# Pseudo-random shifts of the recorded priorities in a planned two-layer trunk kernel

## The chip, the cores and the metric

The kernel runs on one core of a Trainium2 chip. The metric is the device time of one execution in microseconds; the time of a version is the median of its runs. The kernel is one program, planned as a whole before it is emitted: a Python planner decides in which order each engine gets its instructions, and the chip only executes the queues.

## What is computed

Two layers over 1024 tokens of width 1024. Layer 0 mixes tokens by sparse attention (an indexer scores all keys, the 256 best of each query are kept, 16 query heads share 4 key heads); layer 1 mixes them by a gated convolution of width 3. Each mixer is followed by a SwiGLU block of hidden size 2816, and each sublayer has an RMS norm whose shift, scale and gate come from a conditioning vector.

```
def reference(x, c, positions, ada_w, ada_b, ...):
    c_act = jax.nn.silu(c)
    for i in range(DEPTH):
        mod = c_act @ ada_w[i] + ada_b[i]
        sh1, sc1, g1, sh2, sc2, g2 = [m[:, None, :] for m in jnp.split(mod, 6, axis=-1)]
        h = _rmsnorm(x, norm1_g[i]) * (1.0 + sc1) + sh1
        if i % N_MIXERS == 0:
            y = _dsa_mixer(h, positions, ...)
        else:
            y = _short_conv_mixer(h, conv_w_in[j], conv_w[j], conv_w_out[j])
        x = x + g1 * y
        h = _rmsnorm(x, norm2_g[i]) * (1.0 + sc2) + sh2
        x = x + g2 * _swiglu(h, ffn_w_gate[i], ffn_w_up[i], ffn_w_down[i])
    return x
```

## The kernel before

**What is recorded.** Every instruction is first recorded as an `Op` with an estimated cost, its dependences and a priority. 16,676 of them are recorded, in program order. Until the attention is done (up to recorded operation 5433, with a few exceptions) the priority is a due time in estimated microseconds, which the code sets by hand in `plan.pri`: projections are spaced 6.2 apart, attention blocks by `t_att`. In everything after that, the tail, `plan.pri` is None and the priority is the operation's own number, so that an earlier recorded operation goes first.

**What sets the order.** `drain` keeps an estimated clock for each engine. Again and again it takes the engine that could start something earliest and gives it, of the operations whose inputs are ready by that estimated clock, the one of the lowest priority (`choice` may prefer, on TensorE, one that keeps the array's tile shape, within 4.0 of priority). Since readiness comes from the estimated clock, one operation that moves shifts the clock of its engine a little, and later picks fall differently, also among operations whose own priority has not changed. Some PSUM copies may go to ScalarE or VectorE; `drain` decides that too. The order found is what the five hardware queues get, and each queue is worked off in that order. SyncE (SP) issues nearly all DMAs, so a DMA that waits for its buffer holds those behind it.

**How the matmuls are done.** A float32 product is three matmuls: operands are split into a high and a low part (`split`: ScalarE casts `whi`, VectorE subtracts for `wlo`), and `mm3` multiplies hi*hi, hi*lo, lo*hi. In the tail each product of two 2x2 blocked matrices is done with seven block products instead of eight (`Pair.done` for the weights of the convolution, gate and up; `down_pairs` for down). For one `Pair` SP loads two weight tiles `raw` (there are two buffers), VectorE forms sums of their blocks (`s<-raw`, `s<-raw,s`), ScalarE and VectorE split each sum into `whi` and `wlo`, TensorE runs 12 matmuls of 128x512 for each of the seven products, and VectorE adds the products up (`u`, `v`, `cv`). A `raw` buffer is free for the next load when its last sum has been formed. In `conv` VectorE also runs the taps of the convolution on the same tiles, as operations with `vec` as an input. `norm_stat` sums squares over eight tiles on VectorE (`u<-u`), then TensorE transposes the sum (`ps_mm<-ident,u`); its matmuls and those of the neighbouring products stand in one TensorE queue.

**Stages by time in the profile.** Startup, norm and positions to about 100 us; projections and indexer to 297; attention to about 600; output projection and first FFN gate/up to about 1085; down to 1290; convolution to 1500; its output projection to 1590; second FFN to the end.

Of the kernel before, what the change touches and what calls it, by code (L numbers as in the profile page):

```python
# [185 lines left out]
class Plan:  # L186
# [7 lines left out]
    CHANGE = {(ROWS, None): 0.285, (None, ROWS): 0.115, (None, COLS): 0.12, (COLS, None): 0.15,  # L194
              (ROWS, COLS): 0.277, (COLS, ROWS): 0.278}
    TRAIL = 1.0 / 450e3
    STAY = 4.0

    def __init__(self, nc, tc):
# [89 lines left out]
    def matmuls(self, calls, rate, start=True, stop=True):  # L289

        kw = {"start": start, "stop": stop}
        emits = [self.emitter("tensor", "matmul", c, kw) for c in calls]

        def emit():
            for e in emits:
                e()

        self.count += 1
        op = Op("tensor", rate * calls[0][0].free, emit, (self.pri, self.count))
        op.form = tuple(calls[0][1].shape)  # L300
        outs = [c[0] for c in calls]
        self.note(op, [r for c in calls for r in c], outs)
        return op

    def record(self, eng, fn, args, kw, other=None):
        vals = list(args) + list(kw.values())
        outs = [kw["out"] if "out" in kw else args[0]]
        if "accum_out" in kw:
            outs.append(kw["accum_out"])
        refs = [v for v in vals if isinstance(v, Ref)]  # L310
        ins = [v for v in refs if not any(v is o for o in outs)]
        emit = self.emitter(eng, fn, args, kw)
        shaped = outs[0] if isinstance(outs[0], Ref) else refs[0]
        func = {"func": args[2]} if fn == "activation" else {}
        cost, lat = self.cost(eng, fn, shaped, ins, {**kw, **func})
        self.count += 1
        pri = (self.count if self.pri is None else self.pri, self.count)
        op = Op(eng, cost, emit, pri, lat)
        if "accum_out" in kw:
            op.late = 0.13 if eng == "vector" else 0.1  # L320
        if other is not None:
            op.other = (other[0], self.cost(*other[:2], shaped, ins, kw)[0],
                        self.emitter(*other, args, kw))
        if fn == "dma_start":
            op.lat = lat + shaped.free * shaped.shape[0] * 4 / 380e3
        self.note(op, refs, outs)
        return op
# [110 lines left out]
    def choice(self, e):  # L438

        now = self.now[e]  # L440
        if e == "tensor" and now[0][1].form != self.form:
            same = [v for v in now if v[1].form == self.form and v[1].end is None
                    and not v[1].parked and v[0][0] < now[0][0][0] + self.STAY]
            if same:
# [41 lines left out]
    def drain(self, *pools):  # L486

        held = []
        while any(p.pending for p in pools) if pools else True:
# [36 lines left out]
            if op.lat:  # L526
                self.dma = max(self.dma, end) + (op.lat - 1.6)
                end = self.dma + 1.6 + (op.lat - 1.6) * 380e3 * self.TRAIL
                if e == "sync":
# [1452 lines left out]
```

## Time and profile before

| what | value |
|---|---|
| time, median of 3 runs | 2274.2 us (2271.48 to 2274.24) |
| the profiled execution | 2273.65 us, span 2271.9 us, granted clock 0.985 |
| instructions in the profile | 32575 |
| VectorE busy | 1903.7 us (84%) |
| ScalarE busy | 1141.0 us (50%) |
| DMA | 353.72 MB, 156 GB/s on average |

The profile's page gives busy time by engine, the chain of work that ended last, and groups of instructions. A view by windows gives the same for stretches of the span: for each engine the busy time and, in brackets, the number of instructions, then the clock that TensorE was granted. All instructions have the line of the one emitting helper (L276), so tiles tell them apart: `ps_g<-t,whi` writes a PSUM tile `ps_g` from the operands `t` and `whi`. PE is TensorE, DVE VectorE, ACT ScalarE, SP SyncE.

### The profile page before, as it was taken

How to read it: one execution, taken by the hardware profiler on the slowest of the kernel's cores; microseconds unless marked ns; L12 is line 12 of the kernel's file. 1: busy time of each engine (PE TensorE's matmuls, PEld its weight loads, DVE VectorE, ACT ScalarE, POOL GpSimd, SP SyncE). 2: the span in 40 equal slices, each digit the busy share in tenths (PEclk: the TensorE clock that was granted, in tenths of full speed). 3: DMA queues.
4: the chain of work that ended last, by engine and by line, in shares of the span. 5: the costliest groups of instructions: out<-in, count | busy, mean ns of one | idle time of the engine just before them, and what ended most of it. 6: DMA issues, size and time to landing. Idle time of an engine off the chain costs nothing.

```text
span 2271.9 us, 32575 instructions
## 1 busy us (share of the span) xinstructions
PE 2199.9 (97%) x11435; PEld 1779.5 (78%) x11435; DVE 1903.7 (84%) x3828; ACT 1141.0 (50%) x2163; POOL 5.2 (0%) x19
## 2 busy tenths in 40 slices
PE   3999999999999999999999999999999999999999
PEld 3757866876888778888888787887887888888887
DVE  7889999798599989887898998986788887767974
ACT  5587899767654323333445552224553333334444
POOL 0000000000000000000000000000000000000000
PEclk6999989999999999999999999999999999999999
DMA  9313333542354665455972354234445532349824
GB/s 309 122 48 89 97 94 107 161 142 96 110 162 123 222 195 183 147 165 177 389 280 85 122 156 138 86 115 158 121 120 177 157 121 89 125 140 382 290 87 139
DMA packets 332317, 353.72 MB, mean 156 GB/s; under 512 B 19289, under 2 KB 216954, under 8 KB 332154
## 3 DMA queue, kind: packets, MB, share of 16 engines
q1 hardware_dynamic: 331944, 351.52, 47.7%
q8 instruction: 89, 1.46, 0.3%
q14 instruction: 74, 0.61, 0.1%
q10 hardware_dynamic: 210, 0.14, 0.0%
HBM read 278.97 MB, written 68.94 MB: 153 GB/s over the span
## 4 chain that ended last, share of the span: by engine, by line
PE 78%; DVE 10%; issue 3%; ACT 2%; DMA 1%; POOL 0%; ACTq 0%; DVEq 0%; POOLq 0%
PE ps_g L276 45%; PE ps_mm L276 31%; PE ps_o L276 2%; DVE u L276 2%; DVE wlo L276 1%; PE ps_L L276 1%; DVE s L276 1%; DVE sc L276 1%; DMA adaw<-in_ada_w_dram 1%; DVE p L276 1%; DVE karena L276 1%; DVE adacc L276 1%; ACT p L276 1%; ACT junk L276 1%; ACT pf L276 0%
## 5 line engine op out<-in xcount | busy, mean ns | idle before, releaser
L276 ACT CAST whi<-raw 128x512 fp32r<-128x512 f32 (+1 forms) x313 | 192.5, 619 | 392.2 <-PE ps_g L276 142.2
L276 PE MATMUL ps_g<-t,whi 128*128 128x512 f32 x1184 | 367.6, 391 | 3.6 <-ACT whi L276 3.6
L276 PE MATMUL ps_g<-h,whi 128*128 128x512 f32 x1056 | 326.3, 390 | 0.5 <-ACT whi L276 0.5
L276 ACT CAST whi<-s 128x512 fp32r<-128x512 f32 x276 | 170.5, 621 | 305.7 <-DVE s L276 130.9
L276 DVE TENSOR_TENSOR wlo<-raw,whi 128x512 fp32r<-128x512 f32 (+1 forms) x314 | 214.3, 684 | 80.7 <-ACT whi L276 80.6
L276 PEld LDWEIGHTS ps_g<-t,whi 128*128 128x128 f32 x1184 | 223.0, 189 | 51.3 <-ACT whi L276 5.3
L276 PE MATMUL ps_g<-t,wlo 128*128 128x512 f32 x592 | 231.6, 392 | 3.5 <-DVE wlo L276 3.3
L276 PEld LDWEIGHTS ps_g<-h,whi 128*128 128x128 f32 x1056 | 197.6, 188 | 41.9 <-ACT whi L276 1.4
L276 PE MATMUL ps_g<-h,wlo 128*128 128x512 f32 x528 | 205.9, 390 | 1.6 <-DVE wlo L276 1.6
L276 DVE TENSOR_TENSOR wlo<-s,whi 128x512 fp32r<-128x512 f32 x276 | 187.4, 684 | 17.3 <-ACT whi L276 16.8
L276 PE MATMUL ps_mm<-t,whi 128*128 128x512 f32 x608 | 189.5, 392 | 1.7 <-ACT whi L276 1.7
L276 PE MATMUL ps_g<-ph,whi 128*128 128x512 f32 x572 | 179.1, 389 | 0.0
L276 PEld LDWEIGHTS ps_mm<-t,whi 128*128 128x128 f32 x608 | 114.8, 189 | 26.4 <-ACT whi L276 2.8
L276 PEld LDWEIGHTS ps_g<-t,wlo 128*128 128x128 f32 x592 | 111.7, 189 | 29.3 <-DVE wlo L276 6.0
L276 PEld LDWEIGHTS ps_g<-ph,whi 128*128 128x128 f32 x572 | 107.4, 188 | 22.3
L276 PE MATMUL ps_mm<-t,wlo 128*128 128x512 f32 x304 | 119.8, 394 | 2.5 <-DVE wlo L276 2.5
L276 ACT ACTIVATE junk<-sc,bs 128x384 bf16<-128x384 f32 (+3 forms) x124 | 109.9, 887 | 15.8 <-DVE bs L276 7.7
L276 PEld LDWEIGHTS ps_g<-h,wlo 128*128 128x128 f32 x528 | 99.1, 188 | 22.7 <-DVE wlo L276 2.1
L276 DVE TENSOR_TENSOR u<-u 128x512 f32<-128x512 f32 x170 | 114.1, 683 | 1.8 <-ACT u L276 0.8
L276 DVE SCALAR_TENSOR_TENSOR adacc<-adaw,cact,adacc 128x512 f32<-128x512 f32 x140 | 104.2, 744 | 8.5 <-DMA adaw<-in_ada_w_dram 8.0
L276 PE MATMUL ps_g<-ph,wlo 128*128 128x512 f32 x286 | 110.3, 389 | 0.0
L276 PE MATMUL ps_mm<-hhi,whi 128*128 128x512 f32 (+2 forms) x240 | 93.5, 391 | 4.7 <-ACT hhi L276 3.1
(310 smaller groups left out, 4769.3 us busy)
## 6 DMA issues: line engine op xcount, KB each, us to landing
adaw<-in_ada_w_dram SPq DMA_DIRECT2D x160, 256.0 KB, 2.9
ph<-in_ffn_w_down_dram SPq DMA_DIRECT2D x66, 512.0 KB, 6.5
raw<-in_ffn_w_gate_dram SPq DMA_DIRECT2D x54, 512.0 KB, 4.2
raw<-in_ffn_w_up_dram SPq DMA_DIRECT2D x54, 512.0 KB, 4.1
raw<-in_conv_w_in_dram SPq DMA_DIRECT2D x34, 512.0 KB, 4.6
raw<-in_ffn_w_down_dram SPq DMA_DIRECT2D x44, 256.0 KB, 2.6
ph<-in_ffn_w_down_dram SPq DMA_DIRECT2D x44, 256.0 KB, 4.3
raw<-in_attn_w_in_dram SPq DMA_DIRECT2D x18, 512.0 KB, 3.7
```

Source lines behind the costliest of these rows:

```text
L276: f(*[a.get() if isinstance(a, Ref) else a for a in args], **{k: a.get() if isinstance(a, Ref) else a for k, a in kw.items()})
```

## The change

A table of 123 seeds is added, one for each hundred recorded operations; 29 of them are not zero, and from operation 12,300 on there is none. Where the seed of its hundred is not zero, an operation's priority gets a fixed pseudo-random amount added: up to 4.0 either way in the tail, that is four places of the recorded order, and up to 0.5 either way where the priority is a due time. Nothing is computed differently, and the operations and their dependences are the same.

```
+    SPAN = 100
+    SHAKE = (0, 824, 0, 0, 0, 657, 0, 545, 0, 210, 0, 0, 0, 0, 0, 240, 0, 214, 0, 0, 0, 0, 0,
...
-        self.count += 1
-        op = Op("tensor", rate * calls[0][0].free, emit, (self.pri, self.count))
+        op = Op("tensor", rate * calls[0][0].free, emit, self.rank())
...
+    def rank(self):
+
+        self.count += 1
+        i, at = self.count // self.SPAN, self.count if self.pri is None else self.pri
+        seed = self.SHAKE[i] if i < len(self.SHAKE) else 0
+        if seed:
+            x = ((self.count * 7919 + seed * 104729) * 2654435761 >> 13) % 1024 / 512.0 - 1.0
+            at += x * (4.0 if self.pri is None else 0.5)
+        return at, self.count
...
-        self.count += 1
-        pri = (self.count if self.pri is None else self.pri, self.count)
-        op = Op(eng, cost, emit, pri, lat)
+        op = Op(eng, cost, emit, self.rank(), lat)
```

What the planner makes of it, over both programs: 2,897 operations have another priority; by the longest common order of each queue, 511 of 10,083 operations stand elsewhere on TensorE, 982 of 3,558 on VectorE, 357 of 1,897 on ScalarE and 66 of 1,123 on SyncE; 26 copies change engine (15 from VectorE to ScalarE, 11 the other way). On TensorE and SyncE nothing is moved after about operation 13,300 (about 1,780 us), nor on SyncE between recorded operations 6,046 and 10,101 (about 650 to 1,296 us).

The helper's line is 276 before and 283 after. Three places follow.

VectorE in the convolution, before: from the sums of one `Pair` to the last of them (1384.0 to 1390.6 us in the profile). `s` are sums of weight blocks and `wlo` low parts, `vec` marks the taps.

```order
L276 TENSOR_SCALAR u<-u,vec 128x512
L276 COPY u<-u 128x2
L276 TENSOR_TENSOR s<-raw,s 128x512
L276 SCALAR_TENSOR_TENSOR u<-u,vec 128x512
L276 TENSOR_TENSOR u<-u 128x512
L276 SCALAR_TENSOR_TENSOR u<-u,vec 128x512
L276 TENSOR_SCALAR u<-u,vec 128x512
L276 TENSOR_TENSOR wlo<-s,whi 128x512
L276 SCALAR_TENSOR_TENSOR u<-u,vec 128x512
L276 TENSOR_TENSOR wlo<-s,whi 128x512
L276 SCALAR_TENSOR_TENSOR u<-u,vec 128x512
L276 TENSOR_TENSOR s<-raw 128x512
```

The same `Pair` on VectorE after the change, from its first sum on:

```order
L283 TENSOR_TENSOR s<-raw 128x512 x2
L283 TENSOR_TENSOR u<-cv,ps_mm 128x512
L283 TENSOR_TENSOR wlo<-raw,whi 128x512
L283 TENSOR_TENSOR v<-u 128x512
L283 TENSOR_TENSOR wlo<-s,whi 128x512
L283 TENSOR_TENSOR v<-v,ps_g 128x512
L283 TENSOR_TENSOR s<-s,raw 128x512
L283 TENSOR_TENSOR v<-v 128x512
L283 TENSOR_TENSOR s<-raw,s 128x512
L283 TENSOR_SCALAR v<-v,vec 128x512
```

The sum `s<-raw` that closed the `Pair` before (last row of the first list) now stands right behind its first one (`x2`), and the other sums stand ahead of the taps.

VectorE in the gate and up products of the second FFN, before (1709.2 to 1715.9 us):

```order
L276 TENSOR_TENSOR s<-s,raw 128x512
L276 TENSOR_TENSOR u<-u,ps_g 128x512
L276 TENSOR_TENSOR s<-raw,s 128x512
L276 TENSOR_TENSOR u<-u 128x512
L276 TENSOR_TENSOR wlo<-s,whi 128x512
L276 TENSOR_TENSOR u<-u,ps_g 128x512
L276 TENSOR_TENSOR u<-u 128x512 x2
L276 TENSOR_TENSOR wlo<-s,whi 128x512
L276 TENSOR_TENSOR cv<-u,cv 128x512
L276 TENSOR_TENSOR s<-raw 128x512
```

and after the change, again from the first sum of the same `Pair`:

```order
L283 TENSOR_TENSOR s<-raw 128x512 x2
L283 TENSOR_TENSOR wlo<-raw,whi 128x512
L283 TENSOR_TENSOR u<-cv,ps_g 128x512
L283 TENSOR_TENSOR wlo<-s,whi 128x512
L283 TENSOR_TENSOR v<-u 128x512
L283 TENSOR_TENSOR s<-s,raw 128x512
L283 TENSOR_TENSOR s<-raw,s 128x512
L283 TENSOR_TENSOR v<-v,ps_g 128x512
L283 TENSOR_TENSOR wlo<-s,whi 128x512
```

Here too the closing `s<-raw` has moved up to the first one, and three sums stand ahead of most `u` and `v`.

TensorE at the norm ahead of the second FFN (1584 to 1588 us): `ps_mm<-ident,u` are the transposes of the sum of squares, the rows ahead of them products of the output projection. Before:

```order
L276 MATMUL ps_g<-rh_15423,whi 128x512 x2
L276 MATMUL ps_g<-rh_15423,wlo 128x512
L276 MATMUL ps_g<-rt_15376,whi 128x512 x2
L276 MATMUL ps_g<-rt_15376,wlo 128x512
L276 MATMUL ps_g<-rt_15376,whi 128x512 x2
L276 MATMUL ps_g<-rt_15376,wlo 128x512
L276 MATMUL ps_g<-rt_15376,whi 128x512 x2
L276 MATMUL ps_mm<-ident,u 128x128 x4
```

After, from the matmul that follows the last one of that list:

```order
L283 MATMUL ps_g<-rt_15376,wlo 128x512
L283 MATMUL ps_g<-rt_15376,whi 128x512 x2
L283 MATMUL ps_g<-rt_15376,wlo 128x512
L283 MATMUL ps_g<-rh_15423,wlo 128x512
L283 MATMUL ps_g<-rh_15423,whi 128x512 x2
L283 MATMUL ps_g<-rh_15423,wlo 128x512
L283 MATMUL ps_g<-rh_15423,whi 128x512 x2
L283 MATMUL ps_g<-rh_15423,wlo 128x512
L283 MATMUL ps_g<-rh_15423,whi 128x512 x2
L283 MATMUL ps_g<-rh_15423,wlo 128x512
L283 MATMUL ps_g<-rt_15376,whi 128x512 x2
L283 MATMUL ps_g<-rt_15376,wlo 128x512
```

Nineteen matmuls that stood behind the transposes now stand ahead of them (the last two, `ps_g<-rt_15376,whi x2`, follow the rows shown).

5 rows, old and new, of the table SHAKE are left out of this document.

## The prediction

> **What bounds the kernel now.** The page first: busy shares, TensorE by slices, the chain that ended last.
>
> ```profile
> span 2271.9 us, 32575 instructions
> PE 2199.9 (97%) x11435; PEld 1779.5 (78%) x11435; DVE 1903.7 (84%) x3828; ACT 1141.0 (50%) x2163; POOL 5.2 (0%) x19
> ...
> PE   3999999999999999999999999999999999999999
> ...
> PE 78%; DVE 10%; issue 3%; ACT 2%; DMA 1%; POOL 0%; ACTq 0%; DVEq 0%; POOLq 0%
> ```
>
> TensorE is the bound: it is idle for 72 us (2271.9 - 2199.9), and the chain runs over it for 78%. The operations stay the same, so an order can only win or lose idle time, and the time of matmuls that run slowly. The second view, busy time by windows, tells where that is:
>
> ```profile
> 0.00:50.00 50.00, 18.34 (x91) 15.50 (x91) 37.38 (x80) 23.57 (x40) 1.76 (x13) 0.71 0.88 313
> 50.00:100.00 50.00, 45.39 (x249) 33.11 (x250) 44.17 (x87) 26.65 (x47) 0.00 (x0) 0.92 0.51 153
> 100.00:297.00 197.00, 192.62 (x1010) 149.29 (x1009) 184.38 (x557) 159.13 (x350) 3.44 (x6) 1.00 0.28 82
> 297.00:375.00 78.00, 72.42 (x536) 44.77 (x536) 76.50 (x291) 75.74 (x218) 0.00 (x0) 0.87 0.33 95
> 375.00:600.00 225.00, 221.57 (x2058) 171.58 (x2059) 181.36 (x556) 170.35 (x343) 0.00 (x0) 1.00 0.36 114
> 775.00:825.00 50.00, 45.39 (x186) 35.52 (x185) 43.52 (x73) 13.92 (x23) 0.00 (x0) 0.93 0.58 184
> 1250.00:1300.00 50.00, 47.14 (x215) 38.36 (x214) 45.11 (x79) 29.49 (x51) 0.00 (x0) 1.00 0.32 106
> 1350.00:1400.00 50.00, 45.79 (x199) 36.58 (x199) 47.13 (x84) 12.06 (x20) 0.00 (x0) 1.00 0.43 127
> 1400.00:1450.00 50.00, 50.00 (x215) 41.18 (x215) 45.57 (x80) 13.15 (x22) 0.00 (x0) 0.97 0.39 119
> 1450.00:1500.00 50.00, 49.00 (x213) 39.40 (x212) 44.11 (x76) 13.13 (x22) 0.00 (x0) 1.00 0.36 103
> 1550.00:1600.00 50.00, 47.49 (x211) 38.44 (x210) 35.80 (x61) 23.94 (x43) 0.00 (x0) 1.00 0.37 121
> 1700.00:1750.00 50.00, 48.47 (x211) 39.19 (x210) 39.29 (x65) 15.39 (x26) 0.00 (x0) 1.00 0.56 171
> 1850.00:1900.00 50.00, 50.00 (x222) 41.42 (x221) 35.73 (x58) 16.68 (x29) 0.00 (x0) 1.00 0.34 106
> ```
>
> The columns after the window's length are PE, PEld, DVE, ACT and POOL, then granted clock, DMA share, GB/s. The last row is a full window: busy 50.00, 222 matmuls. Fewer than 222 in a tail window is lost time, even where busy says 50.00 (busy hides slow matmuls), at the pace of the full stretches:
>
> ```profile
> 1373.80 5.46 PE ps_g L276 x24
> ...
> 1390.01 0.61 DVE s L276
> ...
> 1391.11 6.22 DMA raw<-in_conv_w_in_dram
> 1397.34 0.02 issue
> ...
> 1397.41 0.63 ACT whi L276
> 1398.04 0.04 issue
> 1398.09 0.73 PE ps_g L276 x2
> ```
>
> 24 matmuls in 5.46 us are 0.2275 us each. So the windows from 1250 on lack 7, 23, 7, 9, 11 and 11 matmuls: 1.6, 5.2, 1.6, 2.0, 2.5 and 2.5 us, 15.4 in all, at five places. The first 50 us load weights (DMA share 0.88) and wait; 100 to 375 us have VectorE busy for 260.9 of 275 us.
>
> **The change part by part.** It removes and adds no operation; it moves them.
>
> *Convolution, 1350 to 1450 (6.8 us lost).* The chain above says why: the sum `s<-raw` at 1390.01 frees the weight buffer, the load issued then takes 6.22 us, and TensorE starts again at 1398.09. VectorE was not waiting for that sum's inputs; it had other work ahead of it:
>
> ```profile
> 1384.47 0.68 DVE L276 TENSOR_TENSOR s<-raw,s 128x512 f32<-128x512 f32 x1
> 1385.08 0.74 DVE L276 SCALAR_TENSOR_TENSOR u<-u,vec 128x512 f32<-128x512 f32 x1
> ...
> 1387.40 0.68 DVE L276 TENSOR_TENSOR wlo<-s,whi 128x512 fp32r<-128x512 f32 x1
> ...
> 1389.93 0.68 DVE L276 TENSOR_TENSOR s<-raw 128x512 f32<-128x512 f32 x1
> ```
>
> By the first pair of lists of the change, this sum now stands right behind the first of its `Pair` instead of 24 places later (the first list shows the last 12), some 14 us at 0.6 us a row, so the load can be issued well before 1390. The three sums and two low parts also pass the taps. SP's list has the loads ahead of more of the `cv` fetches, none of which stood in their way before. The stalls grouped by tile in 1350 to 1402 are one on `whi` and one on `wlo`:
>
> ```profile
> L276 PE MATMUL ps_g<-t,whi 128*128 128x512 f32 x64 | 21.1, 410 | 2.4 <-ACT whi L276 2.4
> L276 PE MATMUL ps_g<-t,wlo 128*128 128x512 f32 x31 | 12.7, 411 | 1.5 <-DVE wlo L276 1.5
> ```
>
> Both should go, 3.9 us; so should the slow matmuls behind the first:
>
> ```profile
> 1394.00:1398.00 4.00, 1.69 (x8) 1.07 (x6) 2.26 (x6) 0.58 (x1) 0.00 (x0) 1.00 1.05 347
> 1398.00:1403.00 5.00, 4.90 (x13) 3.54 (x14) 5.00 (x10) 1.29 (x4) 0.00 (x0) 0.66 0.47 167
> 1403.00:1408.00 5.00, 5.00 (x23) 4.07 (x23) 4.12 (x8) 1.78 (x3) 0.00 (x0) 1.00 0.79 210
> ```
>
> Behind the gap the granted clock is 0.66 and 13 matmuls fit where 23 do afterwards: 10 x 0.2275 = 2.3 us more. What is late next is VectorE: 1350 to 1500 leaves it 13.2 us idle (150 - 47.13 - 45.57 - 44.11), and the taps that were passed still have to be done. I take 5.5 of the 6.8 us, and 1.0 of the 2.0 at 1450 to 1500, where sums and low parts pass taps again. Bounds 0 and 8.8.
>
> *Clock, by a page.* The Trainium skill, "TensorE: Matmul & The Clock Gate", Part 1, has the clock halve after an idle window of about 3.4 us; here the rows show 0.66 behind a shorter gap, so the trace is harsher than that rule. By the page alone the 2.3 us would not hang on this stall, and the term would be 3.2 instead of 5.5, the sum 2263.5.
>
> *Second FFN, 1700 to 1750 (2.5 us lost).* The same pattern in its chain:
>
> ```profile
> 1715.31 0.61 DVE s L276
> ...
> 1716.42 7.08 DMA raw<-in_ffn_w_up_dram
> ```
>
> The closing sum stands 14 rows earlier by the second pair of lists, some 8 us; SP issues the two `up` loads ahead of four other DMAs. I take 2.0; bounds 0 and 2.5.
>
> *Norms, 1550 to 1600 and 1250 to 1300 (2.5 and 1.6 us).* TensorE's queue is held by the transposes:
>
> ```profile
> 1585.66 0.70 DVE u L276
> ...
> 1586.46 0.70 DVE u L276
> ...
> 1587.20 0.66 PE ps_mm L276 x4
> ```
>
> TensorE stands meanwhile, from about 1585.6 to 1587.2. Nineteen matmuls now stand ahead of these transposes, 19 x 0.2275 = 4.3 us, over twice the wait, and the `wlo` that they need pass `xr` and `u` on VectorE. At 1298 it is 12 matmuls, but 0.7 us of `adacc` is put ahead of a `wlo` there. I take 2.0 and 1.0; bounds 0 and 4.1.
>
> *775 to 825.* The lists of SP and VectorE are the same there, so its loss stays; it is the one large stall of the tail that isn't touched. 0.
>
> *0 to 600.* Startup waits for loads that can't come earlier: 0. Between 100 and 375 us VectorE is the bound, with 14.1 us idle; TensorE's own idle is 4.4 + 5.6, and 3.4 from 375 to 600. Moves of half a unit shuffle index products, rotary, top-k bits and scores within a few rows. Four copies net leave VectorE for ScalarE, about 0.6 us each, most of them after 450 where VectorE has 20% idle. From these rows: at best all of VectorE's idle time (-14), at worst a loss as dear as the one from 1350 to 1500, the nearest stage where VectorE is as full (+8.8). I take -1, near none, since this stage has moves in both directions.
>
> Sum: 5.5 + 1.0 + 2.0 + 2.0 + 1.0 + 0 + 1.0 = 12.5 us. The profiled execution took 2273.65 us (span 2271.9 and 1.75 around it), so 2261.1; the median of the runs shown is 0.55 higher, and I forecast **2261.5**.
>
> **The rivals.**
>
> *The gain is handed back in the convolution.* The passed taps come back as late `cv` and `u` buffers, VectorE being 94 and 91% busy in the two windows (47.13 and 45.57 of 50), and only FFN, norms and front stay: 2273.65 - 6 = 2268, up to 2271. Against it: VectorE is at 36 of 50 by 1550.
>
> *Slower.* VectorE works its list in order. The sums that were moved up read a weight tile that may not have landed; then everything behind them waits, TensorE's supply too. The trace has such a case:
>
> ```profile
> 804.55 0.75 DVE L276 SCALAR_TENSOR_TENSOR adacc<-adaw,cact,adacc 128x512 f32<-128x512 f32 x1 [0.95 <-DMA adaw<-in_ada_w_dram]
> ...
> raw<-in_conv_w_in_dram SPq DMA_DIRECT2D x34, 512.0 KB, 4.6
> ```
>
> Between a closing sum, which frees a buffer, and the first sum on its next contents stood 10, 9, 3 and 7 rows before, counted in the two programs at the places of the lists; now 12, 31, 11 and 17. Eleven rows are 6.6 us at 0.6. A load that lands later than that holds VectorE: at the 7.08 us of 1716 by 0.5 us, and at 7.7 by 1.1. With 1.1 us in each of the 12 `Pair`s of the convolution and of some 8 `Pair`s of the second FFN before the last moved row, 22 us, less the 12.5 gained: 2283. The point from which it decides is a landing of about 6.6 us. For it: the stalls' landings were 6.2 and 7.1; against it: the median landing is 4.6, and the rows in between have become more.
>
> The Trainium skill says the same of the queue: "PSUM — Partial Sum Buffer", Engine vs sequencer instructions, "ScalarE/VectorE/GpSimdE queues are strict FIFO"; the row with the 0.95 us wait agrees.
>
> *The moves are too small.* Stock in the queues evens four places out: 2273 (within 2 us). Against it: the lists show 24, 14 and 19 places.
>
> *The front gives more.* VectorE's idle time shrinks by half, 7 us, and the five places give all of their 15.4: 2273.65 - 22.4 = 2251.
>
> **How the numbers follow.** Forecast (2252 to 2268) 0.55; handed back 0.17; too small 0.09; slower 0.10; more 0.09. Range 2249 to 2275: it takes in the first three and most of the last, and leaves out the slower case and the far ends of the bounds. This kernel's measurement can tell about 0.2% (4.5 us) from no change, so faster is below 2269.7: 0.55 + 0.09 + half of the case handed back, 0.73 after rounding; the same 0.17; slower 0.10.
>
> **What would show it.** After: windows of 1350 to 1450 with 440 or more matmuls (414 now) and no granted clock below 1.0 there; `s<-raw` of a `Pair` in one go in the timeline, with no DMA wait above 1 us; no chain piece `DMA raw` of 6 to 7 us at the three places; no PE gap at the transposes. It is wrong if 775 to 825 changes by more than 2 us, if the projections end later than 297, if the attention's end (about 600) moves by more than 5 us, or if `s` waits for DMA in the convolution.

## The result, and the profile after

The changed kernel takes **2258.47 us** (median of 4 runs, 2257.06 to 2260.06), the kernel before, run beside it, 2273.94 (median of 4, 2271.48 to 2274.24): a ratio of 0.9935, 95% interval 0.9917 to 0.9952. That is 15.5 us less by the medians, and 13.6 by the two profiled executions (2260.06, the slowest of the four, against 2273.65). The forecast was 2261.5.

The page of the changed kernel, its first rows and the head of its chain of work:

```profile
span 2258.2 us, 32572 instructions
...
PE 2194.4 (97%) x11435; PEld 1777.6 (79%) x11435; DVE 1904.7 (84%) x3824; ACT 1140.7 (51%) x2167; POOL 5.3 (0%) x19
...
PE 84%; DVE 8%; ACT 3%; issue 3%; DMA 2%; ACTq 0%; POOL 0%; SPq 0%; DVEq 0%; POOLq 0%
```

TensorE has the same matmuls and the same share; four operations net have gone from VectorE to ScalarE. TensorE's idle time fell from 72.0 to 63.8 us (2258.2 - 2194.4); the other 5.5 us are busy time, matmuls that no longer run slowly. The chain lies on TensorE for 84% instead of 78.

To place the gain, each stage is cut at the same matmuls in both traces. The view by windows of before, from the attention's end on (the last output projection and first FFN's start, the stall at 800, the long full stretch, the norm of 1300, the convolution, the norm of 1590, the second FFN):

```profile
602.68:705.00 102.32, 102.32 (x636) 92.56 (x636) 89.56 (x153) 60.86 (x104) 0.00 (x0) 1.00 0.52 160
...
775.00:826.00 51.00, 46.39 (x190) 36.35 (x189) 44.52 (x75) 13.92 (x23) 0.00 (x0) 0.93 0.57 181
826.00:1253.72 427.72, 427.31 (x1893) 353.21 (x1893) 363.07 (x586) 170.29 (x292) 0.00 (x0) 1.00 0.60 203
1253.72:1312.00 58.28, 55.42 (x254) 45.15 (x253) 53.30 (x96) 35.92 (x62) 0.00 (x0) 1.00 0.44 139
1352.04:1500.28 148.24, 143.03 (x617) 115.72 (x617) 135.04 (x236) 37.55 (x64) 0.00 (x0) 0.99 0.40 118
1535.41:1626.92 91.51, 89.00 (x394) 72.81 (x394) 63.90 (x104) 41.85 (x72) 0.00 (x0) 1.00 0.43 138
1690.00:1777.14 87.14, 85.61 (x375) 69.96 (x375) 72.34 (x117) 29.89 (x49) 0.00 (x0) 1.00 0.56 174
```

and of the changed kernel:

```profile
598.92:702.20 103.28, 102.47 (x635) 92.44 (x636) 89.78 (x153) 60.31 (x104) 0.00 (x0) 1.00 0.54 162
...
772.20:823.40 51.20, 46.19 (x190) 36.07 (x189) 43.55 (x74) 14.14 (x24) 0.00 (x0) 0.93 0.58 180
823.40:1251.24 427.84, 427.43 (x1894) 353.06 (x1893) 363.48 (x587) 170.22 (x292) 0.00 (x0) 1.00 0.61 203
1251.24:1310.00 58.76, 56.78 (x253) 46.39 (x252) 50.80 (x91) 33.89 (x58) 0.00 (x0) 0.97 0.44 135
1350.08:1492.46 142.38, 140.69 (x618) 114.64 (x617) 134.57 (x236) 38.73 (x65) 0.00 (x0) 1.00 0.40 119
1527.60:1615.84 88.24, 88.24 (x394) 73.04 (x394) 63.57 (x104) 41.87 (x72) 0.00 (x0) 1.00 0.45 143
1679.00:1763.68 84.68, 84.68 (x375) 70.14 (x374) 73.00 (x119) 30.28 (x51) 0.00 (x0) 1.00 0.55 172
```

The second count in a row, matmuls, is equal to within one in each pair, so the lengths compare like with like. The start and attention end 3.8 us earlier (602.68 - 598.92); then come +1.0, +0.2, +0.1, +0.5, **-5.9** for the convolution, **-3.3** for the norm of 1590 and **-2.4** for the second FFN. The last two stages are now full: 88.24 of 88.24 us and 84.68 of 84.68. Behind them nothing differs (0.1 us to the end).

Why the convolution is shorter shows on SP. The timeline of its queue before, where the two loads behind the closing sum of 1390 are issued:

```profile
1390.64 1.01 SPq L276 DMA_DIRECT2D raw<-in_conv_w_in_dram  x2
```

and after, the same two loads:

```profile
1375.42 3.69 SPq L283 DMA_DIRECT2D raw<-in_conv_w_in_dram  x2
```

The closing sum now runs at 1373.2, right behind the `Pair`'s first one, and the first of the loads leaves 15 us earlier, 13 by the stage's own clock (25.3 us behind its start instead of 38.6). The row merges two issues: the second load leaves at 1378.72, 12 us earlier than before (1391.11). Before, the closing sum was the last reader of both tiles of the `Pair`; now that it stands early, `s<-raw,s` at 1378.01 is the last reader of one of them, and the second load waits for that. The loads do not end the chain any more; the chain of the changed kernel over that stretch is TensorE alone:

```profile
1364.84 5.44 PE ps_g L283 x24
1370.28 2.72 PE ps_mm L283 x12
1373.00 8.16 PE ps_g L283 x36
1381.16 2.72 PE ps_mm L283 x12
```

### The profile page after: what moved, and what is told of

Its sections match the earlier page's. It is cut to its first block, busy times and chain, and to the rows that moved or that the text cites. A ratio compares the mean times of both kernels' runs of the same rounds, so it can differ in the third digit from the quotient of the medians.

```text
span 2258.2 us, 32572 instructions
## 1 busy us (share of the span) xinstructions
PE 2194.4 (97%) x11435; PEld 1777.6 (79%) x11435; DVE 1904.7 (84%) x3824; ACT 1140.7 (51%) x2167; POOL 5.3 (0%) x19
## 4 chain that ended last, share of the span: by engine, by line
PE 84%; DVE 8%; ACT 3%; issue 3%; DMA 2%; ACTq 0%; POOL 0%; SPq 0%; DVEq 0%; POOLq 0%
PE ps_g L283 46%; PE ps_mm L283 34%; PE ps_L L283 2%; PE ps_o L283 2%; DMA adaw<-in_ada_w_dram 1%; DVE s L283 1%; DVE u L283 1%; DVE sc L283 1%; DVE wlo L283 1%; DVE adacc L283 1%; DVE karena L283 1%; ACT junk L283 0%; DVE p L283 0%; DVE hlo L283 0%; ACT karena L283 0%
## 5 line engine op out<-in xcount | busy, mean ns | idle before, releaser
L283 ACT ACTIVATE junk<-sc,bs 128x896 bf16<-128x896 f32 (+3 forms) x124 | 109.8, 885 | 17.5 <-DVE bs L283 7.9
L283 DVE SCALAR_TENSOR_TENSOR adacc<-adaw,cact,adacc 128x512 f32<-128x512 f32 x140 | 104.5, 747 | 15.8 <-DMA adaw<-in_ada_w_dram 15.4
L283 PE MATMUL ps_mm<-ph,whi 128*128 128x512 f32 x308 | 96.9, 389 | 0.0
```

The lines of the kernel that those rows point to most:

```text
L283: f(*[a.get() if isinstance(a, Ref) else a for a in args], **{k: a.get() if isinstance(a, Ref) else a for k, a in kw.items()})
```

## The experiments

Every experiment was profiled, and its stages cut at the same TensorE instructions, paired in program order. This table gives each stage's length less that of before's profile, in us, the ends of before's stages at the top; its last column is where the last matmul ended. The medians and ratios stand with each experiment.

| run | to 603 | 776 | 826 | 1254 | 1352 | 1535 | 1627 | 1777 | end | all |
|---|---|---|---|---|---|---|---|---|---|---|
| changed kernel | -3.8 | +1.0 | +0.2 | +0.1 | +0.5 | -5.9 | -3.3 | -2.4 | -0.1 | -13.6 |
| front only | -3.4 | 0.0 | -0.7 | +0.6 | -1.4 | -3.6 | -1.6 | +0.1 | -0.3 | -10.4 |
| one sum | +1.4 | +0.1 | 0.0 | 0.0 | 0.0 | -3.7 | -0.2 | -0.4 | -0.5 | -3.4 |
| sum back | -5.2 | 0.0 | +0.1 | +0.1 | +0.6 | +0.1 | -3.3 | -2.4 | -0.5 | -10.5 |
| transposes | +0.6 | 0.0 | -2.4 | +1.0 | 0.0 | +0.2 | -1.6 | +0.2 | +0.4 | -1.7 |
| sums early | +2.2 | +1.4 | -6.4 | +0.9 | +0.5 | -8.2 | 0.0 | -1.3 | +0.4 | -10.5 |
| numbers plus 1 | -1.7 | +4.2 | -0.6 | +0.5 | -0.7 | +0.5 | -3.3 | -1.4 | -0.5 | -3.1 |
| numbers plus 2 | -1.1 | 0.0 | -0.8 | +0.3 | +0.5 | -2.3 | -3.3 | -1.9 | +0.2 | -8.4 |
| picked | -0.9 | 0.0 | -2.3 | -0.8 | -1.4 | -3.2 | -3.3 | -2.4 | -0.5 | -14.7 |
| front, two numbers | +1.3 | 0.0 | -2.2 | +1.1 | -0.7 | +1.3 | -1.6 | +0.5 | 0.0 | -0.3 |
| combined | -0.4 | +2.0 | -6.2 | +1.5 | -0.9 | -6.5 | -3.3 | -1.3 | +0.1 | -15.0 |
| closing sums only | -0.7 | +0.2 | -8.8 | +0.4 | -0.2 | -5.8 | -3.1 | -2.3 | -0.2 | -20.5 |
| changed, again | -5.0 | 0.0 | -2.2 | +1.3 | +0.6 | -6.9 | -3.3 | -2.4 | -0.5 | -18.4 |

### Only the front's numbers

```
+    SHAKE = (0, 824, 0, 0, 0, 657, 0, 545, 0, 210, 0, 0, 0, 0, 0, 240, 0, 214, 0, 0, 0, 0, 0, 0,
+             0, 0, 0, 0, 0, 190, 28, 0, 0, 0, 0, 0, 0, 974, 0, 0, 0, 0, 0, 683, 0, 0, 0, 0, 0, 0,
...
+             0, 0, 0, 0, 0, 0, 0, 0, 0, 0, 0, 0, 0, 0, 0, 0, 0)
```

> Only the numbers of the first 5,200 operations are kept (start, projections, attention); all later ones are 0. On every engine the order up to the attention's end is then that of the changed kernel; from there to the convolution it is that of before, but for five swaps of neighbours. In the convolution, without a number there, the planner still puts the closing sum of 1390 us 30 places ahead, and at the norm of 1590 us 8 matmuls ahead of the transposes; the second FFN is as before. Theory (what counts is where the closing sums and the transposes stand, whatever put them there): front -3.8 us, the same as in the changed kernel's trace, convolution -5 to -6, norm of 1590 -1 to -1.8, second FFN 0: a profiled execution near 2263, ratio 0.995. Rival (each stage's gain needs the numbers given to that stage): only the front's 3.8, so 2270, ratio 0.998. Rival (the order in the front does nothing, its 3.8 us are chance): convolution and norm alone, 2267.

Measured: 2264.4 us, ratio 0.9963 (0.9953 to 0.9973). Front -3.4, norm of 1590 -1.6, second FFN +0.1 as the theory had it; the convolution gave 3.6, less than the 5 to 6 foretold, with new gaps of 1.3 us at 1349 and 1.4 at 1432; the norm of 1300 gave 1.4 that was not foretold. A stage whose hundreds carry no number thus gained 3.6 us because operations that ran some 800 us ahead of it had been moved: what counts is the place the planner ends up with. (How far a stage's time can differ without any move, the run with the numbers plus 2 shows below: 2.3 us.)

### One closing sum alone

```
+    MOVE = {10684: -60.0}
...
-        return at, self.count
+        return at + self.MOVE.get(self.count, 0.0), self.count
```

All numbers of the table are 0 here. Recorded operation 10684 is the closing sum of 1390 us.

> All numbers 0, so the order of before, but the closing sum of the convolution's stall at 1390 us (one operation) is given a place 60 earlier in the order of record; it then stands 24 places earlier on VectorE, and what follows in the convolution is reshuffled a little (the next closing sum but two falls 24 places back). Theory: this one sum frees the weight buffer in time, and the stall of 2.6 us, the one of 1.7 in front of it and the slow matmuls behind it go: the convolution is 5 to 7 us shorter, nothing else moves (2267 to 2269, ratio 0.9975). Rival (the gain is the sum of many moves, taps and fetches included): less than 2 us. Rival (handed back): the other closing sum, now 24 places late, makes the same stall at about 1421, and the sum is 0.

Measured: 2270.66 us, ratio 0.9990 (0.9980 to 0.9999). In the profile the convolution is 3.7 us shorter and every other stage behind the front within 0.5. The stall of 2.6 us and its slow matmuls are gone; gaps of 1.5 and 1.1 us, both on `wlo`, are left in front of it, and a gap of 1.4 us at 1438 is new: the other closing sum, which fell back, runs at 1433.0, its loads leave from 1433.7 on, and ScalarE can split the tile only at 1439.4. So this one sum carries 3.7 of the 5.9 us, and the rival of handing back is right in part. One priority was changed, but the planner moved many of the stage's VectorE rows with it.

### The closing sum held back

```
+    HOLD = {10684: 10622}
...
+        self.held[self.count] = op
+        if self.count in self.HOLD:
+            self.link(self.held[self.HOLD[self.count]], op)
```

> The changed kernel with all its numbers, but the closing sum of 1390 us is held behind the last of the taps that stood ahead of it before; it and what follows it in the convolution then stand within a few places of before (3 to 8 instead of 10 to 33), and the rest of the kernel is in the changed kernel's order. Theory: the convolution gives back 5 to 6 us, with a load of about 6 us at the end of its chain and a granted clock below 1.0 behind it; all other stages keep the changed kernel's times: 2266 profiled, ratio 0.9965. Rival (the sum doesn't matter, the other 150 rows that move do): less than 2 us given back, 2261.

Measured: 2266.67 us, ratio 0.9966 (0.9955 to 0.9978). The convolution is back at before's length (+0.1), all of the 5.9 us, and norm and second FFN keep -3.3 and -2.4. The chain of this run has the pattern of before again, load and all:

```profile
1387.88 0.61 DVE s L284
...
1388.98 5.28 DMA raw<-in_conv_w_in_dram
1394.26 0.02 issue
```

and its windows show the granted clock falling behind the gap:

```profile
1385.00:1389.00 4.00, 2.40 (x13) 1.80 (x11) 4.00 (x7) 0.43 (x1) 0.00 (x0) 1.00 0.26 66
1389.00:1393.00 4.00, 3.33 (x9) 2.34 (x10) 3.29 (x8) 0.19 (x1) 0.00 (x0) 0.71 0.86 234
```

With the run before it, this shows the cause of the stall and of the slow matmuls behind it: the buffer that is freed late. The 5.9 us are not the price of that sum alone, though, since the rows behind it went back to within a few places of before too.

### The transposes alone

```
+    MOVE = {11920: 73.0, 11921: 72.0, 11922: 71.0, 11923: 70.0}
```

The table is 0, the last line of `rank` as in the run with one sum.

> All numbers 0, but the four transposes of u at the norm of 1590 us are put 73 places later in the order of record, so that 18 matmuls that stood behind them stand ahead (19 in the changed kernel). Theory: the stage from 1535 to 1627 us is 2.5 to 3.3 us shorter (before lost 0.7, 0.7 and 1.6 us there and the changed kernel's is 3.3 shorter); everything else is as before to 0.1 us: 2271 profiled. Rival (the wait moves on: norm, its chain on VectorE and the second operand are later by the same time): 0, or a new gap behind the 18 matmuls of 1 us or more.

Measured: 2272.03 us in the profiled execution. The stage is 1.6 us shorter, not 2.5 to 3.3:

```profile
1534.77:1624.63 89.86, 88.80 (x395) 72.87 (x394) 63.84 (x104) 41.44 (x72) 0.00 (x0) 1.00 0.46 140
```

The gap of 1.6 us at the transposes is gone and no new one came. The two others of the stage, 0.65 and 0.74 us at 1578.6 and 1579.8, stand where before had them; TensorE waits there between products of `rh`, and in the changed kernel other products stand ahead of these. Six profiles of the table have the changed kernel's TensorE order in this stage; all lack the three gaps and gained 3.1 to 3.3. The front-only run, with 8 matmuls ahead of the transposes instead of 18, gained the same 1.6: 8 x 0.2275 = 1.8 us are enough to cover that wait.

### All sums early, without any number

```
         def total(x, y, op):
             s = tail.s4()
+            plan.lead = 60.0
             plan.tt(s, x, y, op)
+            plan.lead = 0.0
...
-        return at, self.count
+        return at - self.lead, self.count
```

> All numbers 0; instead each of the four sums of every Pair is given a place 60 earlier in the order of record, by one rule. In the convolution the closing sums stand 6 to 29 places earlier than before (29 at the stall of 1390 us), in the second FFN 1 to 14 (14 at 1715), in the first FFN too; norms and the front as before. Theory (closing sums early free the buffers early): convolution -5 to -7 us, second FFN -1.8 to -2.4, the stall of 775 to 825 changed by up to 2 either way, front and transposes as before: 2263 to 2266 profiled. Rival (the moves of the random numbers are needed, the sums alone are worth the 3.7 of the one-sum run): 2268 to 2270. Rival (slower, the prediction's: sums moved up find a tile that hasn't landed and hold VectorE): the shortest distances from a closing sum to the first sum on the next contents are 8 to 10 rows here as before; with 1 us of waiting in each of some 30 Pairs 2290 and more.

Measured: 2263.42 us, ratio 0.9957 (0.9942 to 0.9972). Convolution -8.2, more than foretold, the stage of the stall at 800 -6.4, where at most 2 either way had been foretold; the second FFN only -1.3: its stall at 1724 is gone, but a gap of 1.0 us appears at its start (1674). The slower rival fails by the time. The waits ahead of the sums on the convolution's loads, in the answer for the tile `s` from 1350 to 1500, were before (us, times)

```profile
its engine sat idle before it (us, times) until:
  DMA raw<-in_conv_w_in_dram: 5.2, 4
```

in the changed kernel

```profile
  DMA raw<-in_conv_w_in_dram: 2.2, 3
```

and in this run

```profile
  DMA raw<-in_conv_w_in_dram: 2.6, 5
```

So in the convolution sums that are asked for earlier wait less, not more. That doesn't hold everywhere: from 600 to 1900 us, all weight loads together, the sums waited 17.3 us for loads before, 21.8 in the changed kernel and 19.2 in this run (on the gate weights 8.8, 15.2 and 14.5). Most of the increase is in the second FFN, from 3.3 to 12.0 us in the changed kernel, where TensorE never stops.

### Other numbers: each plus 1, each plus 2

```
+    SHAKE = (0, 825, 0, 0, 0, 658, 0, 546, 0, 211, 0, 0, 0, 0, 0, 241, 0, 215, 0, 0, 0, 0, 0, 0,
...
```

```
+    SHAKE = (0, 826, 0, 0, 0, 659, 0, 547, 0, 212, 0, 0, 0, 0, 0, 242, 0, 216, 0, 0, 0, 0, 0, 0,
...
```

> The changed kernel with 1 added to each number that isn't 0: the same hundreds are moved by the same rule, by other amounts. The planner leaves the closing sum of 1390 us 2 places from where it was, and those of the second FFN too; at the norm of 1590 us 20 matmuls come ahead of the transposes. Theory (places, not numbers): convolution within 1.5 us of before, second FFN 0 to -0.4, norm of 1590 -1.6 to -3.3, front not foretold by any place (within 5 of before either way): 2266 to 2276 profiled, likeliest 2271. Rival (moving priorities by chance helps as such, it loosens the lists): about the changed kernel's gain, 2260.

> The changed kernel with 2 added to each number that isn't 0. On every engine the convolution has the order of before, row by row; the second FFN has the order of the changed kernel, row by row; at the norm of 1590 us 20 matmuls come ahead of the transposes; the front has an order of its own. Theory: convolution 0 (its 2.6 us stall and slow clock back), second FFN -2.4, norm of 1590 -1.6 to -3.3, front within 5 either way: 2264 to 2274, likeliest 2269. Rival (the gain of a stage depends on when the stages ahead end, since DMA and lists drift against each other): second FFN by over 1 us off -2.4, or convolution by over 1 us off 0.

Measured, plus 1: 2268.31 us, ratio 0.9979 (0.9969 to 0.9990). Where the sums stayed, the convolution stayed (+0.5); the norm of 1590 gave 3.3; the second FFN gave 1.4, more than foretold; and a new wait of 2.7 us in the output projection (630 us) with the slow matmuls behind it cost 4.2. These other chance moves, one draw, won a third of what the table's did by the medians.

Plus 2: 2264.56 us, ratio 0.9962 (0.9947 to 0.9977). The norm of 1590 gave 3.3, the second FFN 1.9 (2.4 was foretold, 0.4 is lost ahead of it). But the convolution, whose rows are before's one by one, was 2.3 us shorter, so its rival holds there: the same order has another price in another execution. A gain of this size in one profile of the convolution is thus no proof of a better order. The windows around the stall in this run:

```profile
1394.00:1398.00 4.00, 2.62 (x10) 1.46 (x10) 3.30 (x6) 1.24 (x2) 0.00 (x0) 1.00 0.83 290
1398.00:1402.00 4.00, 4.00 (x18) 3.09 (x18) 4.00 (x8) 1.69 (x3) 0.00 (x0) 1.00 0.60 203
```

and in the run with the transposes alone, which has the same rows there:

```profile
1394.00:1398.00 4.00, 1.29 (x6) 0.63 (x4) 1.98 (x5) 1.04 (x2) 0.00 (x0) 1.00 0.88 309
1398.00:1402.00 4.00, 3.98 (x11) 2.90 (x11) 4.00 (x8) 0.41 (x2) 0.00 (x0) 0.63 0.59 193
```

A gap of 1.4 us was followed by the full clock and 18 matmuls in 4 us, one of 2.9 us by a clock of 0.63 and 11.

### Two numbers of the front

```
+             0, 190, 28, 0, 0, 0, 0, 0, 0, 0, 0, 0, 0, 0, 0, 0, 0, 0, 0, 0, 0, 0, 0, 0, 0, 0, 0,
```

All other numbers are 0.

> Only the numbers of the 29th and the 30th hundred of operations are kept (attention, some 360 to 385 us into before), all others 0: start and projections have the order of before, the attention's lists change from there on (505 rows of TensorE, 153 of VectorE), the convolution's closing sum of 1390 us stays. Theory (the front's gain arises where ScalarE, not VectorE, is the full engine, 366 to 412 us: copies change between the two engines there): from 375 us to the attention's end 2 to 3 us shorter, projections as before but for their own spread of about 1.5 us: 2270 profiled. Rival (the gain stems from the numbers of the projections, which shift everything behind): 0 to 1 us, 2273.

Measured: 2273.61 us in the profiled execution. The attention end is 1.3 us later than before's, so the theory falls. Windows of this run, cut where the matmuls of both rows together agree with before's (1163):

```profile
353.11:408.60 55.49, 54.58 (x500) 41.49 (x500) 46.92 (x151) 52.94 (x123) 0.00 (x0) 1.00 0.43 125
408.60:484.70 76.10, 73.30 (x663) 60.80 (x664) 66.91 (x199) 55.06 (x114) 0.00 (x0) 1.00 0.47 146
```

Before:

```profile
352.73:412.04 59.31, 57.40 (x508) 42.02 (x508) 50.49 (x167) 56.36 (x130) 0.00 (x0) 1.00 0.40 126
412.04:483.32 71.28, 70.92 (x655) 60.19 (x656) 62.21 (x185) 51.17 (x104) 0.00 (x0) 1.00 0.49 149
```

The first row is 3.8 us shorter (with 8 of its matmuls fewer), the second 4.8 longer. ScalarE is indeed the fullest helper in the first (56.36 of 59.31 us), but the move of two hundreds won nothing on the whole. Where the front's 3.8 us come from is left open.

### Putting parts together

Three versions keep the numbers of the front and those from 11,600 on; all between are 0. The first moves seven operations of the first FFN besides, three sums and four `adacc` steps (`adacc` adds up the product of the conditioning vector with the weights `adaw`):

```
+    MOVE = {6504: -60.0, 6519: -60.0, 6534: -60.0, 6561: 120.0, 6563: 120.0, 6565: 120.0, 6567: 120.0}
```

> The numbers of the first 5,200 operations and of those from 11,600 on are kept, all between are 0; besides, three sums of one Pair of the first FFN (closing sum at 794 us) get a place 60 earlier and four adacc steps beside them 120 later, so that the closing sum stands some 15 rows earlier, its weight loads ahead of two adaw loads on SP, and the adacc steps behind the sums. Theory, stage by stage from the runs so far: front -3.4 to -5.2, 600 to 775 us 0, 775 to 825 -3 to -4.9 (the whole of what is lost there), norm of 1300 -1.4, convolution -3.6, norm of 1590 -3.3, second FFN -2.4: -17 to -20, so 2254 to 2257 profiled, ratio 0.992. Rival (stages drift against each other): a stage falls short by over 1 us, 2258 or more. Rival (the stall of 775 to 825 is bound by DMA, not by the order): that stage stays within 1 us of before, 2259.

Measured: 2257.12 us, ratio 0.9929 (0.9914 to 0.9944). Norms, second FFN as foretold, convolution nearly; the front gave only 0.9 in this profile, so the rival that a stage falls short by over 1 us came true (2258.95 profiled), and the stall at 800 only moved: gaps of 0.7, 2.0 and 0.6 us from 786 to 792 with a clock of 0.50 behind them (-2.3 instead of -3 to -4.9).

> The sums of every Pair early by the one rule, and the numbers of the first 5,200 operations and of those from 11,600 on kept, all between 0. The first FFN has the order of the run with the sums early, the front and the norm of 1590 us that of the changed kernel. Theory, stage by stage from the runs so far: front -3 to -5, first FFN with its stall -3 to -4.5, norm of 1300 -1.4 to +0.5, convolution -7 to -8.5, norm of 1590 -3.3, second FFN -1.2, the end within 0.5: -18 to -22, so 2252 to 2256 profiled, ratio 0.991. Rival (the stages' gains don't add, since each starts at another phase of the loads): the changed kernel's 2258 to 2260, ratio 0.9935.

Its edit is the one of "all sums early" besides those numbers. Measured: 2256.21 us, ratio 0.9922 (0.9908 to 0.9936). The profiled execution, 2258.94, is where the rival had it, the median at the upper end of the theory's 2252 to 2256. Most of the stages add, the front gave 0.4, and four waits on `wlo` are new, of 1.2, 0.7, 2.3 and 1.0 us at 705, 836, 1349 and 1670. The timeline of VectorE ahead of the longest:

```profile
1348.85 0.70 DVE L282 TENSOR_TENSOR s<-raw 128x512 f32<-128x512 f32 x1
...
1351.25 0.70 DVE L282 TENSOR_TENSOR wlo<-raw,whi 128x512 fp32r<-128x512 f32 x1
```

Four sums of the `Pair` stand ahead of the low part that its first product needs. By the recorded order only the last of them frees buffers, which gave the third version:

```
-        p7 = self.product(s3(total(a11, a21, ALU.subtract)), "t3")
+        plan.lead = 60.0
+        s4 = total(a11, a21, ALU.subtract)
+        plan.lead = 0.0
+        p7 = self.product(s3(s4), "t3")
```

> As the combined run, but only the closing sum of a Pair (the last of its four) is moved 60 places earlier, not the three before it. The closing sums stand 15 to 33 places earlier than in before nearly everywhere in the first FFN and the convolution; the low parts wlo that were late in the combined run, at 705, 836, 1349 and 1670 us, stand 2 to 7 places earlier than before instead of 3 or 4 later there; from a closing sum to the first sum on the next contents there are 9 to 35 rows instead of 8 to 21. Theory (the last reader of a buffer early and nothing else): the combined run's stalls of 1.2, 0.7, 2.3 and 1.0 us on wlo go, all else as there: 4 to 5 us below it, 2251 to 2254 profiled, ratio 0.990. Rival (what is late next takes it, VectorE being full in the convolution): within 1.5 us of the combined run, 2256 to 2259.

> The changed kernel once more, on the same chip as the run with the closing sums alone, for comparison. Theory: every stage behind the attention within 0.1 us of its first profile but the one from 775 to 826, where loads decide; start and front within 2: 2258 to 2262 profiled, ratio 0.9935. Rival (stages drift with the front's end): convolution or second FFN differ by over 1 us from the first profile.

Measured on one chip: **2253.07 us**, ratio 0.9910 (0.9896 to 0.9923), against 2259.35, ratio 0.9939 (0.9926 to 0.9951), for the changed kernel again. The version with the closing sums alone beats both kernels, by 0.3% over the changed one: its slowest of five runs, 2254.03, is below the changed kernel's fastest of five, 2255.07. Against the combined run, taken on another chip, the intervals of the ratios overlap, so that step is shown by its profile alone: the four waits are gone, and the stall at 800 too, where TensorE is full now:

```profile
775.10:816.75 41.65, 41.65 (x187) 34.04 (x186) 40.21 (x69) 12.94 (x22) 0.00 (x0) 1.00 0.70 217
```

against 51.00 us for 190 matmuls before. The changed kernel's second profile repeats the first to 0.1 us in the norm of 1590, the second FFN and the norm of 1300, but not in the convolution (-6.9 against -5.9), the stall at 800 (-2.2 against +0.2) and the front (-5.0 against -3.8).

## Why the prediction was right, point by point

**The median and the bound.** 2258.47 lies 3.0 us below the forecast, inside its own range (2252 to 2268), and TensorE's idle and slow time is what changed, as foretold. The sum was 12.5 us, the profiles show 13.6. That they are so close is in part luck: front, norm of 1590 and second FFN gave 4.5 us more than was taken, convolution, norm of 1300, 775 to 826 and the stretch behind the attention 3.3 less, and the second profile of the same kernel shows 18.4. Most signs held: the clock is 1.00 in both windows from 1350 to 1450, no `DMA raw` piece is left in the chain at the three places and no gap at the transposes, and the projections end 1.9 us earlier.

**Convolution, 5.5 + 1.0 taken, 5.9 measured.** The step holds: with the closing sum held back everything returned, the slow matmuls included; with it alone moved up, 3.7 came. The split of the rest is not settled. Where one sum was moved alone, two waits on `wlo` and a gap of 1.4 us behind the next closing sum but two were left, which the changed kernel does not have; but the closing sums of all `Pair`s, without any other sum moved, gave 5.8 as well. And one order alone differs: before and two profiles with its rows here (transposes, numbers plus 2) gave 0, +0.2 and -2.3. Two of the signs that were named came out differently: the windows of 1350 to 1450 hold 432 matmuls, not 440, as gaps of 0.9 (1352), 0.7 and 0.5 us (1439 and 1440) are left; and a sum does wait for its load, 1.09 us (it waited in before too, 5.2 us in all, so that sign could not tell the kernels apart):

```profile
1372.60 1.29 DVE L283 TENSOR_TENSOR s<-raw 128x512 f32<-128x512 f32 x2 [1.09 <-DMA raw<-in_conv_w_in_dram]
```

TensorE had work throughout (the chain above), so that sign was set too strictly: what VectorE loses while TensorE's supply lasts costs nothing.

**Norm of 1590, 2.0 taken, 3.3 measured.** The place was right, its size was not. The transposes are worth 1.6; 1.4 more are the two waits at 1579 and 1580, which the window's 2.5 us held as well but the step did not name. The last 0.3 is not placed.

**Second FFN, 2.0 taken, 2.4 measured**: right, and the stage is full. No run moved its closing sum alone; the run with the sums early, which has no number, lost the stall too, and the front-only run, with before's rows here, kept it (+0.1).

**Norm of 1300, a gain of 1.0 taken, a loss of 0.5 measured.** The failing step is that the `adacc` ahead of a `wlo` was priced as idle time alone. The wait at the transposes, 1.39 us, is gone as foretold; the one on `wlo` grew from 1.80 to 2.15, so 1.0 us less was idle. But behind the two gaps the clock had stayed at 1.00, and behind the longer one it fell, which was in no term and cost 1.5; the windows of the changed kernel:

```profile
1289.00:1293.00 4.00, 2.76 (x13) 1.94 (x11) 3.90 (x7) 3.36 (x6) 0.00 (x0) 1.00 0.81 261
1293.00:1297.00 4.00, 3.26 (x8) 2.62 (x9) 4.00 (x8) 1.17 (x3) 0.00 (x0) 0.61 0.17 47
```

The three profiles with these rows lost 0.5 or 0.6 us, and two of the others that lie between (gaps of 2.0 us) went one way each, -0.7 at the full clock and +0.5 with a fall.

**775 to 825, 0 taken, +0.2 measured.** The order is unchanged there and so, in this pair of profiles, is the loss. As a sign it was worthless, though: six runs whose rows there are before's but for one swap of neighbours (front only, one sum, sum back, transposes, two numbers, changed again) gave from -2.4 to +0.1, and those that won 2.2 or 2.4 gave back 1.0 to 1.3 by 871 us. The difference is the clock. Ten profiles have before's TensorE order in this stage: where the clock was at half for 6.83 us, four of them gave 0.0 to +0.2; for 3.41 us, three gave -0.6 to -0.8; where it never fell, three gave -2.2 to -2.4. In before, behind gaps of 1.85 and 1.44 us:

```profile
806.00:810.00 4.00, 3.44 (x8) 2.76 (x9) 4.00 (x7) 2.80 (x5) 0.00 (x0) 0.50 0.31 93
```

and in the run with the transposes alone, behind 1.82 and 1.44 us:

```profile
805.00:809.00 4.00, 2.56 (x10) 1.81 (x11) 3.84 (x7) 1.95 (x4) 0.00 (x0) 1.00 0.34 109
```

**Front, 1.0 taken, 3.8 measured.** This is the mis-sized term: nothing but bounds stood behind it, and 375 to 600 us had been read in one window, where ScalarE's full stretch, from 336 to 394, does not show (the run with two numbers did not find the gain there). One pair of profiles is not enough here: seven profiles with the changed order of the front ended it between 597.5 and 602.3 us (mean 599.9), four with that of before between 602.7 and 604.9 (mean 603.7). The means differ by 3.8. What the order does in the front stays open. The spread among the seven goes with the clock: four were at half clock for 13.7 to 17.1 us between 100 and 600 us and ended by 599.3, three for 20.5 to 30.7 us and ended at 601.8 or later.

**Out of every term:** +1.0 us from 603 to 705, one wait of TensorE at 654.6 on a norm's transposes, which stood behind an `adaw` load of 5.7 us by the chain. Two later profiles with the same rows there (sum back, changed again) do not have it.

**The rivals.** Slower fell, though not because its step is wrong: the sums' waits on loads shrank from 5.2 to 2.2 us in the convolution but grew from 3.3 to 12.0 in the second FFN, and TensorE did not wait for them there. Handed back fell for the whole change and holds in part for a single sum. Too small fell. That the front gives more was half right: 3.8 of the 7 us, while the five places gave 11.1 (5.9, 3.3 and 2.4 won, 0.5 lost), not 15.4.

## What to carry to other kernels

Where a planner orders the queues, look for the last reader of a scarce buffer and place it by the load that it sets free, not by the product that it feeds: one such sum moved alone won 3.7 us here, and a rule for all such sums, in place of 15 of the table's 29 numbers, beats the whole table by 0.3%. Two neighbours of the table won only a third and half as much: what a shuffle wins is found by measuring it, not by shuffling. Move that reader alone, since the other sums, moved up as well, delayed the low parts that TensorE wanted next (four waits of 0.7 to 2.3 us). Before a stage is credited with a gain, repeat the profile with an unchanged order: a full stage repeats to 0.1 us, one with waits differs by 1 to 5.

## What the runs showed of the hardware

The granted clock falls behind gaps of 1.6 to 2.9 us, and not by their length alone. At the norm of 1300 gaps of up to 1.80 us kept 1.00 in nine profiles; one of 1.96 us kept it in one and was followed by 0.57 over the next 4 us in another; three of 2.14 or 2.15 us were followed by 0.57, 0.57 and 0.61. A gap of 2.31 us at 1352 in the combined run kept 1.00, one of 1.65 us at 1389 in the run with two numbers did not.

What decides can be read from the clock records of the traces. From 600 us to 2240 us, in the fourteen profiles, the clock fell 18 times, each time to 0.50, for 3.41 or 6.83 us. Within a profile the falls start whole multiples of 3.41 us apart (numbers plus 1: 632.34, 809.84 and 1400.34, 177.50 and 590.50 us apart, 52 and 173 times 3.413), so the clock is set on a fixed grid, wherever the gaps lie. In the 3.41 us ahead of each fall TensorE had been busy, by its instructions in the trace, for 28 to 50%; of 6,689 other such stretches at the full clock only three were below 50% (46, 48 and 49%). So a stretch about half idle is enough here, and a gap costs no clock when the grid splits it. The price was 1.5 us at the norm of 1300 (a fall of 3.41 us), and 2.2 to 2.4 at 800 (6.83 us), of which 1.0 to 1.3 came back behind the stage.

The Trainium skill, "TensorE: Matmul & The Clock Gate", Part 1, has the clock halve after an idle window of about 3.4 us and calls the window free-running. The second agrees with the grid of 3.41 us. The first does not, if it means a window without any work: in these rows TensorE was busy for up to half of it.

The other surprise is how well a full stretch repeats: from 898 to 1254 us, where TensorE never stops, ten of the thirteen other profiles agree with before's to 0.05 us, and three differ by 0.1, 0.3 and 0.8, though the whole programs differ by up to 20 us.
